# The head of a two-layer hybrid backbone: all four modulation halves on the tensor engine, strictly ordered loads, and a context projection begun with half the features

## The chip, the cores and the metric

The kernel runs on one core of a Trainium2 chip. The metric is the device time of one execution in microseconds; the median of several runs is compared. A core has a tensor engine (PE in the profile, with PEld for its weight loads), a vector engine (DVE), a scalar engine (ACT), GpSimd (POOL) and a sync engine (SP), here the issuer of nearly all transfers; 16 DMA engines carry them.

## The reference, cut to what matters

Two layers work on 1024 latent tokens with 256 context tokens in front, 1024 features each, in fp32. Layer 0 attends globally and in a window, layer 1 has a convolution and a neighbourhood attention. The change lies where layer 0 begins:

```python
m = silu(cond) @ mod_w[l] + mod_b[l]          # cond: c for latent, c_ctx for context
shift, scale, gate = split(m, 3)              # 1024 features each
h = rms_norm(x, norm_g[l]) * (1 + scale) + shift
aq, ak, av, ag, bq, bk, bv, bg = split_cols(h @ w_in, EVEN_WIDTHS)
```

`mod_w[0]` is 1024 x 3072. Before any token of layer 0 can be projected, 1024 x 2048 of it (shift and scale, 8.4 MB) are read and multiplied by two vectors.

## The kernel before, in words

Everything is kept with features on partitions: eight feature tiles of 128 (`dk` 0 to 7). Tokens come in three chunks (`CHUNKS`): chunk 0 is the context (256 tokens), 1 and 2 are 512 latent tokens each. A projection in fp32 precision is made of three matmuls (`mm3`, L319) on a high and a low part of both operands: hi x hi, hi x lo, lo x hi. The high part is a copy on ACT, the low part a subtraction on POOL or DVE (`split`, L296).

Each chunk's `h` is made in four steps. `norm_x` squares the eight tiles on ACT and adds them on DVE; `rstd_steps` (L246) sums over partitions on PE, takes the power -1/2 on POOL with a Newton step on DVE, and spreads the result over the partitions with PE (L263). `make_h` (L303) multiplies each tile by scale and norm on DVE (L308), adds the shift on ACT, and splits. `HV` says per tile whether DVE (v) or POOL (g) makes the low part.

Shift (part 0) and scale (part 1) are computed in halves of 512 features, each from four tiles of 512 KB. `mod_half` (L171) uses PE: the two condition vectors are the stationary operand, 16 instructions (L180); the row of 512 results is copied by ACT (L182), transposed by four small matmuls (L185), and DVE adds the bias (L189) and, for scale, forms `gs` (L191). `mod_half_v` (L195) multiplies and adds on DVE (L216, L221) and sums over partitions with PE (L227). The same function later makes the gate of layer 0 and the modulation of layer 1, one step per `tick` (L742) of the layer-0 projections; `solo` is true until the first QKV projection and its first gate blocks are done.

The head's order is written as a string:

```python
PLAN = 'p0mvnbwmm1h2nbhnbh'
MWR = "ABxAVx"
```

`0`, `1`, `2` load chunks, `m` and `v` are modulation halves on PE and on DVE, `n` and `b` are the norm and its spread, `w` loads the first QKV weights, `h` makes a chunk's `h`. The halves are taken in the order shift 0, shift 1, scale 0, scale 1; the second one goes to DVE. `MWR` names the buffers in which modulation weights land, in turn: A and B are the key buffers, V the value buffer of the attention that follows, x a pool of the head. `mw_tile` (L151) hands them out. `after_mod(k)` holds a transfer on its issuing queue behind the last k modulation loads. Beyond that a list scheduler with a timeline model orders each engine's instructions, with the order of the code as priority; `tc.issue_after(i)` makes what follows on i's engine stand behind i there, and makes no other engine wait.

`proj_qkv` (L792) then works through ten token blocks j of 128 (two of context, eight latent), with 24 matmuls of 384 columns each (L320 to L322), calls `tick` at `dk` 1, 4 and 7, and copies the result out on ACT; rotary steps follow on DVE (L828, L830) and POOL (L832), and `qk_tail` (L837) transposes on PE (L840).

Of the kernel before, what the change touches and what calls it, by code (L numbers as in the profile page):

```python
# [18 lines left out]
P = 128  # L19
DK = 8  # L20
# [30 lines left out]
PFB = 2  # L51
MWB, WRB = 2, 2
OHQ = 0
# [36 lines left out]
def tile_kernel(ctx: ExitStack, tc: tile.TileContext, a, out):  # L90
# [57 lines left out]

    mm0 = []

    def mw_tile():  # L151
# [19 lines left out]
    def mod_half(pool, l, part, j):  # L171

        pb = bank("pp", nm("pm"))
        c0 = part * 1024 + j * 512
        for d2 in range(4):
            w2 = mw_tile()
            mm0.append(SY.dma_start(w2, a["mod_w"][l, 2 * d2 * P : (2 * d2 + 2) * P, c0 : c0 + 512].rearrange("(d p) n -> p d n", d=2)))
            for d in range(2):
                dk = 2 * d2 + d
                PE.matmul(pb[0:2, :], csil[:, dk, :], w2[:, d, :], start=(dk == 0), stop=(dk == DK - 1))  # L180
        row = a0.tile([P, 512], F32, tag="ost", name=nm("mrow"), bufs=2)[0:2, :]
        SC.copy(row, pb[0:2, :])  # L182
        tr = bank("tr", nm("trm"))
        for i in range(4):
            PE.transpose(tr[:, 2 * i : 2 * i + 2], row[:, i * P : (i + 1) * P], ident[0:2, 0:2])  # L185
# [3 lines left out]
        VE.tensor_tensor(dst, trv, modb[:, l, o : o + 4, None].broadcast_to([P, 4, 2]), op=ALU.add)  # L189
        if part == 1:  # L190
            VE.scalar_tensor_tensor(gs[l][:, j * 4 : j * 4 + 4, :], dst, 1.0,  # L191
                                    normg[:, l, j * 4 : j * 4 + 4, None].broadcast_to([P, 4, 2]),
                                    op0=ALU.add, op1=ALU.mult)

    def mod_half_v(pool, l, part, j, conds):  # L195

        c0 = part * 1024 + j * 512
        pool, tag, bufs = (kvp, "QH", 3) if mwp[0] is not None else (pool, "macc", 2)
        accs = [pool.tile([P, 512], F32, tag=tag, name=nm("macc"), bufs=bufs) for _ in conds]
        pre = []  # L200
        for dk in range(DK):
            if solo[0] and dk % 2 == 0:
                w2 = mw_tile()
                d_ = SY.dma_start(w2, a["mod_w"][l, dk * P : (dk + 2) * P, c0 : c0 + 512].rearrange("(d p) n -> p d n", d=2))
                if mwp[0] is not None:
                    mm0.append(d_)
                pre = [w2[:, 0, :], w2[:, 1, :]]
# [28 lines left out]
    def newton_rsqrt(pool, v, n, tag):  # L236
# [7 lines left out]
        return r  # L244

    def rstd_steps(pool, accs, n, tag, inv=1.0, tr="tr"):  # L246
# [12 lines left out]
        yield  # L259
        yield  # L260
        bc = bank(tag, nm("bc"))
        for b in range(nb):
            PE.matmul(bc[:, b * P : (b + 1) * P], r[:, b : b + 1].broadcast_to([P, P]), ident, start=True, stop=True)  # L263
        return bc
# [54 lines left out]
    def mm3(o, lh, ll, rh, rl, first, last):  # L319
        PE.matmul(o, lh, rh, start=first, stop=False)  # L320
        PE.matmul(o, lh, rl, start=False, stop=False)  # L321
        done[0] = PE.matmul(o, ll, rh, start=False, stop=last)  # L322

    raws = []
# [329 lines left out]
    with ExitStack() as p0x:  # L654
        w0p = p0x.enter_context(tc.tile_pool(name="w0p", bufs=1, reuse_waits="tile"))
        W0B = 8

        def load_w0(src, u, n):
            return load_w(w0p, a[src], u * n, n, 384, W0B, rb=WRB)

        with tc.tile_pool(name="st0", bufs=1, reuse_waits="tile") as st0:
# [4 lines left out]
            def load_x(c):  # L666
# [4 lines left out]
                else:  # L671
                    t = st0.tile([P, DK, n], F32, tag=f"xr{c}", name=f"xr{c}")
                    xraw[c] = [t[:, dk, :] for dk in range(DK)]
                    for d in range(0, DK, 4):
                        SY.dma_start(t[:, d : d + 4, :],
                                     a["cT"][:, d : d + 4, :] if c == 0 else a["xT"][:, d : d + 4, 0:n])
                    return
                for dk in range(DK):
                    SY.dma_start(xraw[c][dk], a["xT"][:, dk, t0 - 256 : t0 - 256 + n])

            def norm_x(c):
                n = CHUNKS[c][1]
                acc = kvp.tile([P, 512], F32, tag="QH", name=nm("acc"), bufs=3)
                for dk in range(DK):
                    if dk == 0:
                        SC.activation(acc[:, :n], xraw[c][0], AF.Square)
                    else:
                        sq = kvp.tile([P, 512], F32, tag="QL", name=nm("sq"), bufs=3)
                        SC.activation(sq[:, :n], xraw[c][dk], AF.Square)
                        VE.tensor_tensor(acc[:, :n], acc[:, :n], sq[:, :n], op=ALU.add)  # L690
                return acc

            def norm_bc(c, acc):
                n = CHUNKS[c][1]
                return run(rstd_steps(st0, [acc], n, "st"))[:, :n]

            made = [0]
            accs, bcs, mh = [], [], [(0, 0), (0, 1), (1, 0), (1, 1)]
            mwp[0] = st0
            for ev in PLAN:  # L700
                if ev in "012":
                    with after_mod(XA):
                        load_x(int(ev))
                elif ev == "p":
                    SC.dma_start(modb, a["mod_b"])
                    SC.dma_start(normg, a["norm_g"])
                elif ev == "n":
                    accs.append(norm_x(len(accs)))
                elif ev == "w":
                    with after_mod(XA):  # L710
                        w0 = load_w0("ev_qkv", ORDER[0], 384)
                elif ev == "m":
                    mod_half(st0, 0, *mh.pop(0))
                elif ev == "v":
                    run(mod_half_v(st0, 0, *mh.pop(0), (0, 1)))
                elif ev == "b":
                    bcs.append(norm_bc(len(bcs), accs[len(bcs)]))
                elif ev == "h":
                    make_h(0, made[0], lambda dk, c=made[0]: xraw[c][dk], bcs[made[0]], h[made[0]])
                    made[0] += 1  # L720

# [921 lines left out]
```

## Time and profile before

| | |
|---|---|
| median of 3 runs | 1569.27 us (1566.07 to 1572.54) |
| profiled execution | 1571.46 us, span 1569.6 us |
| PE busy over the span | 1460.8 us (93%) |
| DVE / POOL / ACT busy | 1129.4 / 830.0 / 762.0 us |
| granted TensorE clock, mean | 0.961 |
| first QKV matmul | 47.72 us |
| first matmul of latent chunk 1 | 62.01 us |
| moved by DMA | 221.03 MB, mean 141 GB/s |

Engine names are as above; SPq and ACTq are the queues from which transfers are issued. A row of the timeline has start, duration, engine, line, operation, output and inputs, shapes and count, and in brackets how long the engine had been idle and what released it. Rows whose matmuls overlap have durations longer than the distance of their starts.

### The profile page before, as it was taken

The page shows a single profiled execution, that of the slowest core. Times are in us where ns is not written, and L with a number is a line of the kernel's source. Part 1 is how long each engine was busy: PE and PEld are TensorE (multiplying, and loading weights), DVE is VectorE, ACT ScalarE, POOL GpSimd, SP SyncE. Part 2 cuts the span into 40 slices and gives each one's busy share as a digit, 9 for nine tenths or more (in the row PEclk, how much of TensorE's full clock was granted, in tenths as well). Part 3 has the DMA queues.
Part 4 walks back from the last instruction along what each step waited for, and adds up shares of the span by engine and source line. Part 5 has one row for each costly group of instructions (what it writes and reads, how often), then busy time and mean ns, then how long its engine had stood idle before and what let it go on. Part 6 is the DMA issues. An engine that isn't in the chain of part 4 may idle for free.

```text
span 1569.6 us, 22251 instructions
## 1 busy us (share of the span) xinstructions
PE 1460.8 (93%) x6984; PEld 1178.9 (75%) x6984; DVE 1129.4 (72%) x2172; ACT 762.0 (49%) x1545; POOL 830.0 (53%) x762
## 2 busy tenths in 40 slices
PE   6989999998999999899999889999999999899995
PEld 1878877876888677588887568888887787677784
DVE  4898896797768677455488668999654466776776
ACT  2721354545454754655555746443343445545472
POOL 1561463555465675756545756665443333444575
PEclk9899999999999999999999989999999999799897
DMA  9548245424431225612112022214547888889632
GB/s 337 190 142 260 87 142 167 132 67 125 154 116 47 67 91 167 224 47 61 48 38 85 14 94 61 81 58 148 177 154 224 237 229 242 248 231 251 187 95 108
DMA packets 199438, 221.03 MB, mean 141 GB/s; under 512 B 18956, under 2 KB 155352, under 8 KB 199320
## 3 DMA queue, kind: packets, MB, share of 16 engines
q1 hardware_dynamic: 192656, 208.04, 43.5%
q10 hardware_dynamic: 6664, 11.57, 2.3%
q8 instruction: 55, 0.90, 0.2%
q14 instruction: 63, 0.52, 0.1%
HBM read 159.51 MB, written 60.03 MB: 140 GB/s over the span
## 4 chain that ended last, share of the span: by engine, by line
PE 65%; DVE 14%; DMA 11%; issue 4%; POOL 2%; SPq 2%; ACT 1%; ACTq 0%; DVEq 0%; POOLq 0%
PE p L322 6%; PE p L321 6%; PE p L320 6%; PE ov L411 4%; PE ov L413 4%; PE ov L412 4%; PE po L320 4%; PE po L321 4%; PE po L322 4%; PE st L467 4%; PE st L471 4%; DMA mw<-in_mod_w_dram 3%; DVE macc L221 2%; PE pq L322 2%; PE pq L321 2%
## 5 line engine op out<-in xcount | busy, mean ns | idle before, releaser
L301 POOL TENSOR_TENSOR pl<-pf,ph 128x512 fp32r<-128x512 f32 (+4 forms) x321 | 393.7, 1237 | 320.1 <-ACT ph L298 260.0
L301 POOL TENSOR_TENSOR wl<-wr,wh 128x256 fp32r<-128x256 f32 (+2 forms) x256 | 197.5, 788 | 203.1 <-ACT wh L298 192.4
L479 ACT ACTIVATE pf<-st 128x512 f32<-128x512 f32 x284 | 167.3, 597 | 177.4 <-PE st L471 138.3
L298 ACT CAST ph<-pf 128x512 fp32r<-128x512 f32 (+4 forms) x364 | 210.5, 588 | 28.9 <-PE ov L412 21.5
L298 ACT CAST wh<-wr 128x256 fp32r<-128x256 f32 (+2 forms) x264 | 102.8, 404 | 172.9 <-DMA wr<-in_ev_qkv_dram 40.4
L320 PE MATMUL p<-hh,wh 128*128 128x512 f32 x448 | 177.5, 398 | 2.9 <-DVE spk L301 1.5
L321 PE MATMUL p<-hl,wh 128*128 128x512 f32 x448 | 178.0, 398 | 0.2 <-POOL hl L301 0.2
L322 PE MATMUL p<-hh,wl 128*128 128x512 f32 x448 | 175.9, 400 | 0.1
L467 PE MATMUL st<-QH,KAt 128*128 128x512 f32 (+4 forms) x364 | 145.4, 401 | 11.4 <-ACT pf L479 9.7
L411 PE MATMUL ov<-ph,Vt 128*128 128x512 f32 (+4 forms) x364 | 143.5, 394 | 9.7 <-ACT ph L298 5.0
L413 PE MATMUL ov<-pl,Vt 128*128 128x512 f32 (+4 forms) x364 | 144.1, 396 | 6.8 <-POOL pl L301 3.6
L471 PE MATMUL st<-QL,KBt 68*128 68x512 f32 (+4 forms) x364 | 139.0, 391 | 5.8 <-DVE QL L390 5.7
L412 PE MATMUL ov<-ph,Vt 128*64 128x512 f32 (+4 forms) x364 | 140.5, 386 | 0.0
L1122 DVE SCALAR_TENSOR_TENSOR cps<-U,taps,cps 128x512 f32<-128x512 f32 x184 | 124.3, 748 | 0.0
L591 DVE TENSOR_REDUCE mp<-mx 128x1 f32<-128x512 f32 x128 | 85.7, 682 | 42.5 <-PE mx L590 41.8
L221 DVE SCALAR_TENSOR_TENSOR macc<-mw,csil,macc 128x512 f32<-128x512 f32 x107 | 94.5, 901 | 17.5 <-DMA mw<-in_mod_w_dram 16.7
L320 PEld LDWEIGHTS p<-hh,wh 128*128 128x128 f32 x448 | 84.6, 189 | 23.6 <-DVE spk L301 1.7
L321 PEld LDWEIGHTS p<-hl,wh 128*128 128x128 f32 x448 | 84.5, 189 | 20.4 <-POOL hl L301 0.6
L322 PEld LDWEIGHTS p<-hh,wl 128*128 128x128 f32 x448 | 84.8, 189 | 20.1 <-POOL wl L301 0.6
L467 PEld LDWEIGHTS st<-QH,KAt 128*128 128x128 f32 x364 | 71.2, 196 | 33.4 <-ACT pf L479 17.6
L413 PEld LDWEIGHTS ov<-pl,Vt 128*128 128x128 f32 x364 | 71.1, 195 | 32.5 <-POOL pl L301 7.8
L411 PEld LDWEIGHTS ov<-ph,Vt 128*128 128x128 f32 x364 | 71.3, 196 | 27.3 <-ACT ph L298 8.4
(277 smaller groups left out, 3546.2 us busy)
## 6 DMA issues: line engine op xcount, KB each, us to landing
mw<-in_mod_w_dram SPq DMA_DIRECT2D x34, 512.0 KB, 5.9
Q<-qs SPq DMA_DIRECT2D x40, 256.0 KB, 2.7
QH<-Q SPq DMA_DIRECT2D x80, 128.0 KB, 2.8
wr<-in_od_d_dram SPq DMA_DIRECT2D x64, 128.0 KB, 2.7
mw<-in_mod_w_dram SPq DMA_DIRECT2D x28, 256.0 KB, 3.3
wr<-in_ev_qkv_dram SPq DMA_DIRECT2D x32, 192.0 KB, 3.6
KAt<-KD SPq DMA_DIRECT2D x16, 384.0 KB, 6.2
wr<-in_od_wo_dram SPq DMA_DIRECT2D x48, 128.0 KB, 3.2
```

What stands on the lines that cost most here:

```text
L221: VE.scalar_tensor_tensor(t, w, csil[:, dk, q : q + 1], t, op0=ALU.mult, op1=ALU.add)
L298: SC.copy(hi, src)
L301: (GP if leng == "g" else VE).tensor_tensor(lo, src, hi.bitcast(F32), op=ALU.subtract)
L320: PE.matmul(o, lh, rh, start=first, stop=False)
L321: PE.matmul(o, lh, rl, start=False, stop=False)
L322: done[0] = PE.matmul(o, ll, rh, start=False, stop=last)
L411: PE.matmul(o, V[:, 64:192], ph[:, :n], start=(t == 0), stop=False)
L412: PE.matmul(g.ov[0:64, q0 : q0 + n], V[:, 0:64], ph[:, :n], start=False, stop=False)
L413: pvs.append(PE.matmul(o, V[:, 64:192], pl[:, :n], start=False, stop=(last and g.sink is None)))
L467: sts.append(PE.matmul(st[:, :n], KA[:, cs], g.QH[:, q0 : q0 + n], start=True, stop=False))
L471: PE.matmul(st[:, :n], KB[0:68, cs], g.QL[0:68, q0 : q0 + n], start=False, stop=True)
L479: SC.activation(pf[:, :n], st[:, :n], AF.Exp, scale=1.0 if g.bias else SCALE)
```

## The change

All four modulation halves of layer 0 now run on PE, first those of features 0 to 511 (shift, scale), later those of features 512 to 1023. Between them the context is begun: chunk 0's `h` is made for `dk` 0 to 3 (`front`), and its two token blocks run the 24 matmuls that need only those, into two PSUM banks that are kept (`begun`); `proj_qkv` goes on with `dk` 4 to 7 later, with two ticks instead of three for these blocks. Every load of the head goes through `in_turn`, which holds it behind the previous one on its queue. The QKV weights come as two groups of four, with four raw buffers instead of two. The ring of the modulation weights becomes `ABVABVxx`, eight tiles. The back features of chunks 0 and 1 are multiplied by their norm in advance (`scaled`), so that a multiply-add on DVE finishes them when scale and shift are known. `HV0` replaces `HV` in layer 0; `behind` holds PE and ACT instructions in written order around these steps. The second half's bank is "ov", a single one, instead of "pp".

```diff
-MWB, WRB = 2, 2
+MWB, WRB = 2, 4
+HV0 = ('vvvvgvgv', 'gvgvgvgv', 'gvgvgvgv')
-PLAN = 'p0mvnbwmm1h2nbhnbh'
-MWR = "ABxAVx"
-XA = 4
+MWR = "ABVABVxx"
...
+    queue = []
+
+    def in_turn(dma):
+
+        with ExitStack() as cx:
+            if queue:
+                cx.enter_context(tc.issue_after(queue[-1].ins))
+            queue.append(dma())
+        return queue[-1]
...
     def mod_half(pool, l, part, j):
 
-        pb = bank("pp", nm("pm"))
+        pb = bank("ov" if j else "pp", nm("pm"))
...
-            mm0.append(SY.dma_start(w2, a["mod_w"][l, 2 * d2 * P : (2 * d2 + 2) * P, c0 : c0 + 512].rearrange("(d p) n -> p d n", d=2)))
+            mm0.append(in_turn(lambda: SY.dma_start(w2, a["mod_w"][l, 2 * d2 * P : (2 * d2 + 2) * P, c0 : c0 + 512]
+                                                    .rearrange("(d p) n -> p d n", d=2))))
...
-            raws.append(SY.dma_start(raw[:, :nco], src[dk * P : (dk + 1) * P, c0 : c0 + nco]))
+            load = lambda: SY.dma_start(raw[:, :nco], src[dk * P : (dk + 1) * P, c0 : c0 + nco])
+            raws.append(in_turn(load) if mwp[0] is not None else load())
...
+            def scaled(c, bc, dks):
+
+                for dk in dks:
+                    last = VE.tensor_tensor(xraw[c][dk], xraw[c][dk], bc, op=ALU.mult)
+                return last
+
+            def make_h0(c, dks, bc=None):
+
+                cond = 1 if c == 0 else 0
+                for dk in dks:
+                    x = xraw[c][dk]
+                    scale, shift = gs[0][:, dk, cond : cond + 1], modT[0][:, dk, cond : cond + 1]
+                    if bc is not None:
+                        VE.scalar_tensor_tensor(x, x, scale, bc, op0=ALU.mult, op1=ALU.mult)
+                        SC.activation(x, x, AF.Identity, bias=shift)
+                    else:
+                        VE.tensor_scalar(x, x, scale, shift, op0=ALU.mult, op1=ALU.add)
+                    hi, lo = h[c][0][:, dk, :], h[c][1][:, dk, :]
+                    last = SC.copy(hi, x)
+                    (GP if HV0[c][dk] == "g" else VE).tensor_tensor(lo, x, hi.bitcast(F32), op=ALU.subtract)
+                return last
+
+            def start_qkv(w):
+
+                wh, wl = w
+                for j in range(2):
+                    begun[j] = bank("pp", nm("pq"))
+                    for dk in front:
+                        last = mm3(begun[j][:, :384], Hs(h, 0, j * P, P, dk), Hs(h, 1, j * P, P, dk), wh[dk], wl[dk],
+                                   dk == 0, False)
+                return last
...
+            front, back = range(0, 4), range(4, DK)
             mwp[0] = st0
-            for ev in PLAN:
...
+            load_x(0)
+            run(mod_half(st0, 0, 0, 0))
+            known = run(mod_half(st0, 0, 1, 0))
+            bc = norm0(0)
+            scaled(0, bc, back)
+            wf = load_w0("ev_qkv", ORDER[0], 384, front)
+            made = make_h0(0, front, bc)
+            load_x(1)
+            pq = start_qkv(wf)
+            with behind(known, made):
+                bc = norm0(1)
+            spread1 = spread[0]
+            with behind(made):
+                wb = load_w0("ev_qkv", ORDER[0], 384, back)
+            w0 = tuple({**f, **b} for f, b in zip(wf, wb))
+            made, ready = make_h0(1, front, bc), scaled(1, bc, back)
+            with behind(pq):
+                run(mod_half(st0, 0, 0, 1))
+            with behind(spread1):
+                known = run(mod_half(st0, 0, 1, 1))
+            make_h0(0, back)
+            load_x(2)
+            make_h0(1, back)
+            with behind(known, made, ready):
+                bc = norm0(2)
+            make_h0(2, range(DK), bc)
...
-                    pp = bank("pp", nm("pq"))
-                    for dk in range(DK):
+                    d0 = 4 if u == ORDER[0] and j in begun else 0
+                    pp = begun[j] if d0 else bank("pp", nm("pq"))
+                    for dk in range(d0, DK):
```

`norm0` is `norm_x` and the spread in one; `behind(...)` is `tc.issue_after` for each instruction given; `known` and `spread1` are PE instructions, `made` is one of ACT, `ready` one of DVE.

More of the change, by code (lines that the diff above doesn't have):

```diff
@@ L184, in mod_half @@
         for i in range(4):
-            PE.transpose(tr[:, 2 * i : 2 * i + 2], row[:, i * P : (i + 1) * P], ident[0:2, 0:2])
+            last = PE.transpose(tr[:, 2 * i : 2 * i + 2], row[:, i * P : (i + 1) * P], ident[0:2, 0:2])
         trv = tr[:, 0:8].rearrange("p (i c) -> p i c", c=2)
@@ L193, in mod_half @@
                                     op0=ALU.add, op1=ALU.mult)
+        return last
     def mod_half_v(pool, l, part, j, conds):
         c0 = part * 1024 + j * 512
-        pool, tag, bufs = (kvp, "QH", 3) if mwp[0] is not None else (pool, "macc", 2)
-        accs = [pool.tile([P, 512], F32, tag=tag, name=nm("macc"), bufs=bufs) for _ in conds]
+        accs = [pool.tile([P, 512], F32, tag="macc", name=nm("macc"), bufs=2) for _ in conds]
         pre = []
@@ L203, in mod_half_v @@
                 w2 = mw_tile()
[L204 to L206 removed]
+                SY.dma_start(w2, a["mod_w"][l, dk * P : (dk + 2) * P, c0 : c0 + 512].rearrange("(d p) n -> p d n", d=2))
                 pre = [w2[:, 0, :], w2[:, 1, :]]
@@ L244, in newton_rsqrt @@
         return r
+    spread = [None]
     def rstd_steps(pool, accs, n, tag, inv=1.0, tr="tr"):
@@ L262, in rstd_steps @@
         for b in range(nb):
-            PE.matmul(bc[:, b * P : (b + 1) * P], r[:, b : b + 1].broadcast_to([P, P]), ident, start=True, stop=True)
+            spread[0] = PE.matmul(bc[:, b * P : (b + 1) * P], r[:, b : b + 1].broadcast_to([P, P]), ident, start=True,
+                                  stop=True)
         return bc
@@ L322, in mm3 @@
         done[0] = PE.matmul(o, ll, rh, start=False, stop=last)
+        return done[0]
     raws = []
@@ L656, in tile_kernel, with load_w0 @@
         W0B = 8
-        def load_w0(src, u, n):
-            return load_w(w0p, a[src], u * n, n, 384, W0B, rb=WRB)
+        begun = {}
+        def load_w0(src, u, n, dks=range(DK)):
+            return load_w(w0p, a[src], u * n, n, 384, W0B, dks=dks, rb=WRB)
         with tc.tile_pool(name="st0", bufs=1, reuse_waits="tile") as st0:
@@ L690, in norm_x @@
                         VE.tensor_tensor(acc[:, :n], acc[:, :n], sq[:, :n], op=ALU.add)
[L691 to L698, printed above, removed]
-            mwp[0] = st0
-            for ev in PLAN:
[L701 to L720, printed above, removed]
@@ new lines, in norm0 @@
+                return run(rstd_steps(st0, [acc], n, "st", tr="st"))[:, :n]
+            def scaled(c, bc, dks):
[16 more added lines that the diff above has]
+                return last
@@ new lines, in start_qkv, with behind @@
+            def start_qkv(w):
[5 more added lines that the diff above has]
+                                   dk == 0, False)
+                return last
+            @contextmanager
+            def behind(*ins):
+                with ExitStack() as cx:
+                    for i in ins:
+                        cx.enter_context(tc.issue_after(i.ins))
+                    yield
@@ new lines, in tile_kernel @@
+            front, back = range(0, 4), range(4, DK)
+            mwp[0] = st0
+            SC.dma_start(modb, a["mod_b"])
+            SC.dma_start(normg, a["norm_g"])
+            load_x(0)
[9 more added lines that the diff above has]
+                bc = norm0(1)
```

9 lines of the change are left out of this document (5 added, 4 removed).

## The prediction

> **What bounds the kernel now.** I read the busy time by stage first, since the change touches only the head: the stretch up to the end of the first QKV projection. Columns after the window's length: busy us and instruction count of PE, PEld, DVE, ACT, POOL, then granted clock, DMA share and GB/s.
>
> ```profile
> core 0: us, PE busy (x) PEld busy (x) DVE busy (x) ACT busy (x) POOL busy (x), PEclk, DMA share, GB/s
> ...
> 8.90:18.80 9.90, 9.80 (x16) 1.57 (x16) 4.67 (x11) 1.47 (x6) 0.00 (x0) 1.00 1.06 375
> 18.80:23.70 4.90, 0.38 (x4) 0.32 (x4) 4.90 (x10) 2.31 (x5) 1.24 (x1) 0.76 1.05 387
> 23.70:31.20 7.50, 7.45 (x13) 1.16 (x13) 4.71 (x7) 1.01 (x2) 2.41 (x4) 0.70 0.95 325
> 31.20:41.50 10.30, 10.30 (x34) 3.03 (x33) 3.80 (x10) 4.90 (x10) 1.66 (x3) 1.00 1.04 389
> 41.50:47.70 6.20, 3.39 (x29) 3.14 (x28) 5.99 (x15) 5.92 (x14) 1.00 (x1) 0.80 1.05 383
> 47.70:55.20 7.50, 7.14 (x21) 6.31 (x22) 7.50 (x16) 4.34 (x11) 5.84 (x6) 0.50 0.98 338
> 55.20:62.00 6.80, 6.80 (x45) 6.80 (x44) 5.05 (x11) 3.88 (x7) 2.89 (x3) 0.98 0.57 173
> 62.00:78.60 16.60, 16.60 (x99) 16.08 (x99) 14.10 (x21) 12.14 (x25) 10.08 (x10) 1.00 0.08 29
> 78.60:95.30 16.70, 15.35 (x88) 14.50 (x86) 16.70 (x19) 5.15 (x12) 11.01 (x8) 1.00 0.30 90
> 95.30:110.00 14.70, 9.74 (x56) 9.22 (x56) 14.66 (x18) 4.20 (x11) 10.25 (x7) 0.89 0.60 173
> ```
>
> Until 55 us the DMA engines are full, at 325 to 389 GB/s; from 62 us on they are not, and PE and DVE share the load: DVE is busy 45.46 of the 48.0 us after 62. Then I read PE in order of time, to see what it does while the loads run.
>
> ```profile
> 8.93 9.80 PE L180 MATMUL pm<-mw,csil 128*2 128x512 f32 x16 [8.93 <-DMA mw<-in_mod_w_dram]
> 19.49 0.38 PE L185 MATMUL trm<-ident,mrow 2*128 2x2 f32 x4 [0.76 <-ACT mrow L182]
> ...
> 34.52 7.03 PE L180 MATMUL pm<-mw,csil 128*2 128x512 f32 x16
> ...
> 47.72 0.69 PE L320 MATMUL pq<-wh,hc 128*128 128x384 f32 x1 [2.01 <-ACT hc L298]
> 48.21 0.52 PE L321 MATMUL pq<-wl,hc 128*128 128x384 f32 x1
> 48.53 0.52 PE L320 MATMUL pq<-wh,hc 128*128 128x384 f32 x1
> ...
> 62.01 0.34 PE L320 MATMUL pq<-wh,hh 128*128 128x384 f32 x1
> 62.18 0.34 PE L321 MATMUL pq<-wl,hh 128*128 128x384 f32 x1
> ```
>
> One half of the modulation costs PE 9.80 us at the start and 7.03 us later (16 instructions, 0.44 us each). The first QKV matmul starts at 47.72 us. Its successors start 0.32 us apart (48.21 to 48.53), against 0.17 us at full clock (62.01 to 62.18), and the 47.70 to 55.20 window has a clock of 0.50. The context chunk ends where the first latent chunk begins, at 62.01. So the head is two things: 48 us in which PE is fed by loads, and a cold 14.3 us for the 48 context matmuls. The last view is what PE waits for from 62 to 130 us.
>
> ```profile
> PE trk L840 <- DVE qs L301: 5.2, 4, 2.8
> PE trm L227 <- DVE macc L221: 1.8, 1, 1.8
> ```
>
> Those 7.0 us are what an easier DVE could give back. Over the whole span PE has the least slack by far:
>
> ```profile
> PE 1460.8 (93%) x6984; PEld 1178.9 (75%) x6984; DVE 1129.4 (72%) x2172; ACT 762.0 (49%) x1545; POOL 830.0 (53%) x762
> ```
>
> **The change, part by part.** Durations that the steps need, as groups of the first 62 us (mean ns behind the bar):
>
> ```profile
> L690 DVE TENSOR_TENSOR acc<-acc,sq 128x512 f32<-128x512 f32 x14 | 10.8, 770 | 3.9 <-ACT sq L689 3.3
> L221 DVE SCALAR_TENSOR_TENSOR macc<-mw,csil,macc 128x512 f32<-128x512 f32 x14 | 10.6, 794 | 0.0
> L308 DVE SCALAR_TENSOR_TENSOR xr<-xr,gs,bc 128x512 f32<-128x512 f32 x6 | 4.0, 742 | 1.7 <-PE bc L263 1.7
> L690 DVE TENSOR_TENSOR acc<-acc,sq 128x256 f32<-128x256 f32 x7 | 3.7, 527 | 0.0
> L308 DVE SCALAR_TENSOR_TENSOR xr<-xr,gs,bc 128x256 f32<-128x256 f32 x8 | 3.4, 469 | 0.0
> ...
> L189 DVE TENSOR_TENSOR modT<-trm,modb 128x8 f32<-128x8 f32 x3 | 0.5, 155 | 0.0
> ```
>
> ```profile
> L689 ACT ACTIVATE sq<-xr 128x512 f32<-128x512 f32 x14 | 8.3, 620 | 0.4 <-DVE acc L690 0.2 <-DMA xr<-in_xT_dram 0.2
> L298 ACT CAST wh<-wr 128x384 fp32r<-128x384 f32 x8 | 4.0, 510 | 11.4 <-DMA wr<-in_ev_qkv_dram 11.4
> ...
> L314 ACT ACTIVATE xr<-xr,modT 128x256 f32<-128x256 f32 x4 | 1.8, 495 | 0.0
> L182 ACT COPY mrow<-pm 2x512 f32<-2x512 f32 x3 | 1.7, 569 | 6.9 <-PE pm L180 6.9
> L298 ACT CAST hc<-xr 128x256 fp32r<-128x256 f32 x4 | 1.5, 387 | 0.0
> ```
>
> *Loads.* The same bytes go out in another order: context (1.05 MB), shift and scale of features 0 to 511 (4.2 MB), four weight tiles (0.8 MB), chunk 1 (2.1 MB), four weight tiles, the other two modulation halves (4.2 MB), chunk 2 (2.1 MB). At the 375 to 389 GB/s of the full windows, 1 MB takes 2.6 us, so after the first tile at 8.93 the second modulation half is in by about 17 us, the front weights by 19, chunk 1 by 25, the fourth half by 38, chunk 2 by 43. The eight tiles of the new ring hold two halves, so the third half waits only for PE's first one, long done; the queue behind that wait is everything later, in order, and I cost it at nothing because the 4 MB already queued cover it. If that cover were gone, each missed 0.5 MB tile would be 1.4 us. Two raw weight buffers more cost nothing on an engine; they let the back weights be queued as soon as POOL has split the front ones, by about 23 us. The rotary table and the gate weights still stand behind the last four modulation tiles and are first used after 62 us.
>
> *First two halves.* PE starts at 8.93 and ends the first at 18.73 as before, then goes straight on: 7.03 gives 25.8, and two sets of small matmuls (transposes at 0.38 a set, the norm of the context) bring it to 27.0. So PE sets this, not the loads (17 us). The tail is the row copy and the transposes (18.73 to 19.87 in the rows, 1.14), and two DVE instructions of 0.155, with hand-overs 1.6 us; then the feature tile's 0.469 on DVE, 0.495 and 0.387 on ACT: first QKV matmul at about 30.0 us, 17.7 sooner than now.
>
> *Context begun.* 24 of its 48 matmuls. At full clock ACT sets the pace (0.88 per feature tile) and they end near 34; cold (0.32 each) they end at 37.7. PE has had about 3 us of little work, like the 41.50 to 47.70 window, where 3.39 us of small matmuls and a 2.01 us wait were followed by a clock of 0.50. I take 36.8. [...]
>
> *Third and fourth half.* They are put behind the begun context on PE: 36.8 + 7.0 = 43.8. The fourth stands behind the spread of chunk 1's norm as well, and needs the one "ov" bank, which ACT's 0.569 copy frees. The norm: ACT is free of the front tiles near 33, casts four weight tiles (2.0) and squares eight (5.0), to 40; with the last add (0.77), small matmuls, the power on POOL and three small DVE steps it is spread near 43 to 44. So the fourth half runs 44.6 to 51.6, transposes to 52.2, and the same tail puts the first of the remaining context matmuls at about 54.6. This is later than today's 47.72: half the work is done by then, but the one DVE-made half is now 7.0 us of PE.
>
> *Rest of the context.* 24 matmuls, 4.1 us warm, 7.7 cold; middle 5.9, done at 60.5 against 62.01. While PE waits for the second tail (2.6 us) it may take chunk 1's front features, which are ready; how far the written order allows that the trace can't show. Bounds 0 and 2.6; I take 1. So the first latent chunk is 2.5 us ahead.
>
> *DVE and chunk 2.* Gone from DVE: 16 x 0.794 = 12.7 us at most (the two multiplies that start the sums have one input less). Added: eight scaling multiplies, 4 x 0.527 + 4 x 0.770 = 5.2, since the back features are scaled by the norm before their modulation is known; and six instead of four subtractions for the context's low parts, 2 x 0.527 = 1.1. Net 6.4 less. The context's begun half also drops two of the ticks that feed later modulation, 4 x 0.794 = 3.2 us moved behind this stretch. Chunk 2's norm, whose scaling now runs in the DVE-bound stretch after 71 us, can be done by about 70, since its data lands at 43. The rows' 7.0 us of PE waits on DVE are the most this can return; its other end is nothing, as DVE is full of later modulation that moves up into any hole. I take 1.5, nearer to nothing, because that filler stays.
>
> Sum: 2.5 + 1.5 = 4.0 us. The profiled execution took 1571.46 us for a span of 1569.6; from it, 1567.5; from the median 1569.27, which I forecast, **1565**. From the head on, PE is the bound and a shift there should pass through to the end.
>
> **The rivals.** *More than that.* The clock stays up over both short gaps, PE fills the second with chunk 1, and DVE's waits go. Steps: 2.7 and 1.8 us from the two cold stretches, 1.6 more filling, 3 more of the waits: 4.0 + 9.1 = 13 at most, two thirds of it, 9, likely: 1560. For it: the clock was 1.00 from 31 to 41 us with PE busy throughout. Against: the 0.50 after a wait of 2.01. [...]
>
> *No gain, DVE ends it.* The first QKV projection ends when DVE's rope steps and filler let it, wherever the context ended: 1569. For it: 45.46 of 48.0 us busy; against: 6.4 us of DVE work are gone.
>
> *Slower: the fourth half waits for the norm of chunk 1.* Between chunk 1's first square and the spread of its norm the kernel now takes this long:
>
> ```profile
> 36.92 0.62 ACT L686 ACTIVATE acc<-xr 128x512 f32<-128x512 f32 x1
> ```
> ```profile
> 57.25 1.05 PE L263 MATMUL bc<-ident,nr 128*128 128x128 f32 x8
> ```
>
> 20.3 us, with both engines full of other work, where I count 10 to 11. From 33 that is 53.3; the fourth half then runs to 60.4, context matmuls resume at 63.4 and end at about 69.5: 7.5 us behind, 1577. With the second front (chunk 1's features and the third half's row copy on the same ACT queue) a little more. It decides from the point where the spread comes later than 46 us. Against it: ACT has nothing else but weight casts there.
>
> **How the numbers follow.** 0.5% is 7.8 us, about what a measurement of this kernel can tell from no change. Chances: the forecast 0.36; the larger gain 0.27, most of it just past the bound; no gain 0.15; slower 0.22, most of it at the bound or beyond it since the later order may shift too. That gives 0.28 faster, 0.51 within, 0.21 slower. The range takes in the larger gain with part of its excess (1556) and the slow case (1578).
>
> **What would show it.** Right: first QKV matmul near 30 us, a gap of some 3 us on PE before it, 24 context matmuls, then two unbroken halves ending near 52, and the first latent chunk at 59 to 60.5; no DVE instruction of L221's kind before 60. Wrong on the fast side: a clock of 1.00 in the stretch after 30 and latent matmuls before 57. Wrong on the slow side: a PE wait ahead of the fourth half, ended by the norm's DVE or ACT work, or holes in the DMA share before 40 us. Wrong about DVE: the context ends early, but the waits at L840 grow beyond 7 us.

## The result, and the profile after

The changed kernel took 1577.2 us (median; 1573.9 to 1580.1), the kernel before 1567.7 us beside it (1564.6 to 1572.5): a ratio of 1.0056, 95% interval 1.0032 to 1.0081. It is slower by some 9 us; the forecast was 4 us faster. Medians here and below are of each kernel's fast runs, which leaves out one run of the kernel before (2332.63 us) and two each of two kernels further down (160.42 and 161.28; 159.88 and 161.57 us).

The profiled execution after took 1573.93 us (span 1572.1), the fastest of its runs, while the one before (1571.46) was among its slower ones. So the two profiles are only 2.5 us apart, and what they show is read stage by stage, not as a sum. The busy time of PE is as before:

```profile
PE 1459.3 (93%) x6988; PEld 1178.4 (75%) x6988; DVE 1112.4 (71%) x2164; ACT 765.8 (49%) x1551; POOL 836.3 (53%) x761
```

The head by the same windows as in the prediction (busy us and count of PE, PEld, DVE, ACT, POOL, then granted clock, DMA share, GB/s):

```profile
core 0: us, PE busy (x) PEld busy (x) DVE busy (x) ACT busy (x) POOL busy (x), PEclk, DMA share, GB/s
8.90:18.80 9.90, 9.85 (x24) 2.39 (x24) 2.05 (x9) 1.10 (x4) 0.71 (x1) 1.00 1.05 385
18.80:23.70 4.90, 4.90 (x14) 0.95 (x13) 1.41 (x4) 2.10 (x5) 3.86 (x4) 1.00 1.05 386
23.70:31.20 7.50, 4.63 (x19) 2.42 (x18) 3.15 (x10) 3.36 (x9) 0.00 (x0) 0.90 0.97 305
31.20:41.50 10.30, 10.30 (x35) 5.34 (x34) 8.01 (x9) 6.07 (x13) 5.25 (x4) 0.91 1.05 388
41.50:47.70 6.20, 4.60 (x25) 2.56 (x24) 1.77 (x7) 0.75 (x2) 1.01 (x1) 0.92 1.06 380
47.70:55.20 7.50, 7.50 (x15) 1.24 (x13) 7.39 (x11) 6.60 (x12) 3.10 (x2) 0.84 0.90 328
55.20:62.00 6.80, 5.93 (x38) 5.51 (x37) 4.95 (x12) 3.21 (x7) 0.06 (x1) 1.00 0.42 134
62.00:78.60 16.60, 14.88 (x77) 14.09 (x77) 12.08 (x23) 7.96 (x18) 7.47 (x7) 0.90 0.23 72
78.60:95.30 16.70, 15.53 (x92) 15.14 (x91) 16.70 (x19) 9.33 (x19) 12.13 (x9) 1.00 0.26 73
```

PE is now busy from 9 us on but for 2.9 us between 23.7 and 31.2 and 1.6 between 41.5 and 47.7, and from 62 to 78.6 us, where it was busy without a break before, it stands still for 1.7 us. PE in order of time shows where the head lost what it won:

```profile
29.67 0.69 PE L331 MATMUL pq<-wh,hc 128*128 128x384 f32 x1 [2.21 <-ACT hc L727]
30.16 0.52 PE L332 MATMUL pq<-wl,hc 128*128 128x384 f32 x1
30.48 0.52 PE L331 MATMUL pq<-wh,hc 128*128 128x384 f32 x1
...
35.60 7.03 PE L189 MATMUL pm<-mw,csil 128*2 128x512 f32 x16
42.56 1.05 PE L263 MATMUL trs<-ones,acc 128*128 128x2 f32 x8
...
45.55 1.16 PE L273 MATMUL bc<-ident,nr 128*128 128x128 f32 x8 [1.60 <-DVE nr L251]
46.64 8.72 PE L189 MATMUL pm<-mw,csil 128*2 128x512 f32 x16
55.29 0.44 PE L331 MATMUL pq<-wh,hh 128*128 128x384 f32 x1
...
59.68 0.40 PE L195 MATMUL trm<-ident,mrow 2*128 2x2 f32 x4
60.95 1.05 PE L263 MATMUL trs<-ones,acc 128*128 128x2 f32 x8 [0.87 <-DVE acc L706]
61.91 0.44 PE L331 MATMUL pq<-wh,hc 128*128 128x384 f32 x1
...
66.72 0.45 PE L333 MATMUL pq<-wh,hc 128*128 128x384 f32 x1 [1.35 <-DVE hc L728]
```

To 42.6 us all goes as forecast or better. Then the fourth half starts at 46.64 and takes 8.72 us, its transposes stand at 59.68 behind latent matmuls (L331 with `hh`, from 55.29), and the context goes on at 61.91 instead of 54.6. PE's waits from 62 to 130 us, which an easier DVE was to give back:

```profile
PE trm L235 <- DVE macc L229: 3.0, 2, 2.6
PE pq L333 <- DVE hl L728: 1.8, 2, 1.2
PE pq L333 <- DVE hc L728: 1.4, 1, 1.4
PE pq L331 <- ACT hh L727: 0.4, 1, 0.4
PE trk L899 <- DVE modT L236: 0.3, 1, 0.3
```

That is 6.9 us. The same view of the kernel before has one row more than the two that the prediction shows, so its waits come to 7.7 us and not to 7.0:

```profile
PE pq L322 <- DVE hl L312: 0.7, 1, 0.7
```

From here on I use two marks: the first attention matmul, and the first matmul of layer 1's projection. They are the same instructions in every kernel, but the first does not stand for quite the same work: 674 matmuls are recorded ahead of it before, 651 after, 653 with two ticks alone. Before, then after:

```profile
160.06 0.70 PE L578 MATMUL mx<-KAt,QH 128*128 128x256 f32 x4 [0.42 <-DMA V<-vs]
...
929.45 0.40 PE L320 MATMUL p<-hh,wh 128*128 128x512 f32 x1
```
```profile
164.58 1.19 PE L591 MATMUL mx<-KAt,QH 128*128 128x256 f32 x4 [4.30 <-DMA KAt<-K]
...
934.99 0.48 PE L331 MATMUL p<-hh,wh 128*128 128x512 f32 x1
```

The head ends 4.5 us later than before, of which PE waits 4.3 for the first keys; layer 0 takes 770.4 us instead of 769.4; the rest of the span 637.1 instead of 640.2. At the end of the first QKV projection the distance is larger: its last matmul starts at 108.93 us, against 102.20 before.

### The profile page after: what moved, and what is told of

Read it like the earlier page. It is cut to its first block, busy times and chain, and to the rows that moved or that the text cites. A ratio compares the mean times of both kernels' runs of the same rounds, so it can differ in the third digit from the quotient of the medians.

```text
span 1572.1 us, 22248 instructions
## 1 busy us (share of the span) xinstructions
PE 1459.3 (93%) x6988; PEld 1178.4 (75%) x6988; DVE 1112.4 (71%) x2164; ACT 765.8 (49%) x1551; POOL 836.3 (53%) x761
## 4 chain that ended last, share of the span: by engine, by line
PE 71%; DVE 12%; DMA 9%; issue 3%; POOL 2%; ACT 1%; SPq 1%; DVEq 0%; ACTq 0%; POOLq 0%
PE p L331 7%; PE p L332 7%; PE p L333 7%; PE ov L424 4%; PE ov L426 4%; PE ov L425 4%; PE st L480 4%; PE st L484 4%; PE po L331 4%; PE po L332 4%; PE po L333 4%; DVE macc L229 2%; PE pq L331 2%; PE pm L189 2%; PE pq L333 2%
## 5 line engine op out<-in xcount | busy, mean ns | idle before, releaser
L492 ACT ACTIVATE pf<-st 128x512 f32<-128x512 f32 x284 | 167.5, 597 | 186.3 <-PE st L484 137.5
L331 PE MATMUL p<-hh,wh 128*128 128x512 f32 x448 | 180.5, 404 | 5.1 <-DVE spk L312 2.3
L331 PEld LDWEIGHTS p<-hh,wh 128*128 128x128 f32 x448 | 85.6, 191 | 25.5 <-issue 2.8
L229 DVE SCALAR_TENSOR_TENSOR macc<-mw,csil,macc 128x512 f32<-128x512 f32 x92 | 81.4, 901 | 27.0 <-DMA mw<-in_mod_w_dram 23.9
L426 PEld LDWEIGHTS ov<-pl,Vt 128*128 128x128 f32 x364 | 70.3, 193 | 28.1 <-POOL pl L312 9.3
L331 PE MATMUL pq<-wh,hh 128*128 128x384 f32 x256 | 88.3, 345 | 1.2 <-ACT pc L863 0.8
```

The source lines that it names most:

```text
L426: pvs.append(PE.matmul(o, V[:, 64:192], pl[:, :n], start=False, stop=(last and g.sink is None)))
L492: SC.activation(pf[:, :n], st[:, :n], AF.Exp, scale=1.0 if g.bias else SCALE)
```

## The experiments

### First: where in the change does the loss sit?

Theory H: it arises in the head. Rival D: behind the head, since the two ticks left out of the begun blocks push modulation steps into the attention. Four variants of the changed kernel, beside before at 1567.95 us.

**Latent matmuls behind the last transposes.**

```diff
+                        with ExitStack() as cx:
+                            if u == ORDER[0] and not d0:
+                                cx.enter_context(tc.issue_after(known.ins))
                             mm3(pp[:, :384], ...
```

> The changed kernel, with the QKV matmuls of the latent chunks held on PE behind the last modulation transposes, which in the changed kernel stand behind 24 of them (55.29 to 59.68 us). Theory H (the loss is made in the head: PE's written order and the fourth half bring the context's second half at 61.9 us): the context resumes at about 58, the first QKV projection ends 3 to 4 us earlier than the changed kernel's (before 106), total 3 to 5 us less, 1572 to 1574. Rival D (the head is even, the loss comes later, from modulation steps of layer 1 that moved into the attention): the head moves by these 3 us and the total stays at 1576 to 1578.

1588.9 us, 1.0131 (1.0109 to 1.0153): slower than the change itself, and than either theory had it. Attention starts at 166.8 us.

**Three ticks in the begun blocks.**

```diff
-                        if dk % 3 == 1:
+                        if dk % 3 == 1 or d0 and dk == 5:
```

> The changed kernel, with three ticks instead of two for each of the two begun context blocks, so that as many later modulation steps as before are fed into the first projection. Theory H: no change, 1575 to 1579. Rival D: the modulation of the gate and of layer 1 ends earlier again by several us, and the total falls by 4 to 6 us, to 1571 to 1573.

1582.5 us, 1.0081 (1.0055 to 1.0108), above both expectations. The third tick did not bring the time back, so D in this form falls.

**Third half on DVE again** (its loads in turn, its sums in other buffers).

```diff
-            with behind(pq):
-                run(mod_half(st0, 0, 0, 1))
+            run(mod_half_v(st0, 0, 0, 1, (0, 1)))
```

> The changed kernel, with the third half (shift, features 512 to 1023) made on DVE again, so that PE has 7.0 us less to do between the begun context and the fourth half. Theory H: the fourth half starts as soon as chunk 1's norm is spread, at about 42 instead of 46.6 us, the context resumes at about 57, total 4 to 5 us less than the changed kernel, 1571 to 1573. Rival D: 1575 to 1579, or more, since DVE gets 12 us of work back.

1581.7 us, 1.0089 (1.0065 to 1.0113). PE waits 11.1 us while DVE makes the half, and the last transposes come 11 us later than the changed kernel's 59.68 (3.4 of these stand ahead of the wait: this profile's begun context ends at 39.1 instead of 35.7). Made on DVE, the third half costs the head more than on PE:

```profile
50.17 1.87 PE L241 MATMUL trm<-one,macc 128*128 128x2 f32 x8 [11.08 <-DVE macc L235]
...
70.94 0.40 PE L195 MATMUL trm<-ident,mrow 2*128 2x2 f32 x4
```

**No context begun; the whole projection behind the last transposes.**

```diff
-            pq = start_qkv(wf)
...
+                            if u == ORDER[0]:
+                                cx.enter_context(tc.issue_after(known.ins))
```

> The changed kernel without the begun context: all QKV matmuls stand behind the last modulation transposes on PE. Theory H, in its strict form (between 29.7 and 35.6 us PE would otherwise only wait for chunk 1's norm): halves three and four end at about 49, the context runs in one go from about 52 to 61, total within 2 us of the changed kernel, 1575 to 1579. If beginning early pays at all, 4 us for the 24 matmuls and up to 4 more for a cold clock: 1581 to 1585.

1592.9 us, 1.0159 (1.0136 to 1.0182), the slowest of all and above both expectations, with a head that by the first mark is nearly as good as before's:

```profile
160.77 0.71 PE L591 MATMUL mx<-KAt,QH 128*128 128x256 f32 x4 [1.72 <-issue]
...
940.74 0.40 PE L331 MATMUL p<-hh,wh 128*128 128x512 f32 x1
```

Attention starts 0.7 us after before's, and layer 0 then takes 780.0 us instead of 769.4. So H falls too as an account of the whole: its last QKV matmul starts at 107.01 us, 4.8 later than before's, and its head timed alone (below) is 3.1 us longer, but the whole is 25 us slower. Whether the begun context costs the head anything stays open: by the mark this head is 3.8 us better than the changed kernel's (160.8 against 164.6), timed alone it is 1.8 us longer, with four modulation steps more in it.

### Second: single parts on the kernel before

Theory S: the loss behind the head comes from the order that the scheduler writes there, which any change of the head alters. Beside before at 1566.93 us.

**Two ticks for the context blocks, head untouched.**

```diff
-                        if dk % 3 == 1:
+                        if dk % 3 == 1 and (u != ORDER[0] or j > 1 or dk > 1):
```

> The kernel before with one thing altered: the context blocks of the first projection draw the next modulation step two times instead of three, as the begun blocks of the changed kernel do. All work up to 82 us (on PE up to about 130 us) stands in the same order as before, and the head costs the same. Theory S (the loss arises after the head: any change of what comes before makes the scheduler write another order for the attention of layer 0, and the sizes of its stages fit only the order of before): 1575 to 1585 us, the first QKV projection ending within 1 us of before's 102.2, and PE 8 us or more behind before's progress by 380 us. Theory H (what counts is the time of the head): 1566 to 1570, PE never more than 3 us behind.

1566.8 us, 1.0001 (0.9977 to 1.0026). No loss: not every change of the order costs.

**Strict order of the loads alone** (`in_turn` around each load of the head).

> The kernel before with the loads of the head in strict order of the text, and nothing else of the change. The loads already fill the DMA engines to 55 us, so the first QKV matmul stays within 2 us of 47.72 and the first projection ends at 101 to 104. Theory H: 1566 to 1571. Theory S: another order downstream, 1572 to 1585 with the head unchanged.

1581.9 us, 1.0082 (1.0054 to 1.0111). Both expectations had the head unchanged; it is not. With before's plan and ring, a load that waits for a buffer now holds up all behind it: over the first 62 us 280 GB/s are moved instead of 326, and attention starts 15 us late, at 175.2. Here the head's loss did come out at the end.

**All halves on PE alone.**

```diff
-PLAN = 'p0mvnbwmm1h2nbhnbh'
+PLAN = 'p0mmnbwmm1h2nbhnbh'
```

> The kernel before with the second half of the modulation on PE as well, and nothing else of the change: 7.0 us more of PE while it waits for loads, 12.7 us less of DVE. First context spread near 20 instead of 41, first QKV matmul at 44 to 49. Theory H: head 0 to 3 us earlier, 1564 to 1569. Theory S: whatever the head gives, 1572 to 1585.

1572.6 us, 1.0037 (1.0012 to 1.0061): within S's range, but with a head that lost. First QKV matmul at 43.78, attention at 164.6: 4.5 us late, and 5.6 at the end.

**The larger rings alone.**

```diff
-MWB, WRB = 2, 2
+MWB, WRB = 2, 4
-MWR = "ABxAVx"
+MWR = "ABVABVxx"
```

> The kernel before with the ring of eight modulation tiles (which takes turns with the key and value buffers) and four raw weight buffers, and nothing else of the change. Loads are queued earlier, in the same order; the first QKV matmul stays at 46 to 48 us. Theory H: 1564 to 1569. Theory S: 1572 to 1585 with the head unchanged or a little earlier.

1562.2 us, 0.9965 (0.9946 to 0.9985): the only kernel here that beats both, and below both expectations. Not by its head, though:

```profile
44.06 0.44 PE L320 MATMUL pq<-wh,hc 128*128 128x384 f32 x1 [0.70 <-ACT hc L298]
57.22 2.07 PE L263 MATMUL bc<-ident,nr 128*128 128x128 f32 x8
62.05 0.69 PE L320 MATMUL pq<-wh,hh 128*128 128x384 f32 x1 [2.76 <-ACT hh L298]
```

The context starts 3.7 us earlier, but chunk 1's norm is spread when it was before (57.22 against 57.25), PE waits 2.76 for chunk 1, and attention starts 3.3 us later, at 163.3. The time comes from behind the head: layer 0 763.2 us, the rest 634.9.

### Third: the head timed alone, and one number behind it

Theory M: the order behind the head is a matter of its own, and sets most of the loss; H stays the other.

**The cuts.** Kernels cut off behind `fill0(0, w0)`:

```diff
         for _ in fill0(0, w0):
             pass
+        SY.dma_start(out[0:P, 0:256], h[0][0][:, 0, :].bitcast(F32))
+        return
```

> The kernel before cut off behind the first projection and its first gate blocks (about 125 us of its 1570): what follows is left out, and one feature tile is written to the output. It times the head alone, without the attention behind it. Both theories: 120 to 150 us. The difference to the cut of the changed kernel tells them apart, see there.

> The changed kernel cut off at the same place, the rest left out in the same way. Theory H (the whole loss of 9.5 us arises in the head): 8 to 11 us slower than the cut of the kernel before. Theory M (the head loses what PE's progress shows at 110 us, and the rest arises behind it): 2 to 5 us slower. If the head in fact gained, as predicted: 2 us faster or better.

154.38 and 155.76 us: 1.4 us, less than the 2 to 5 that theory M expected. I take it as a lower bound, since the cut ends when DVE has done the modulation steps drawn so far, and the two cuts hold unequal numbers of them:

```profile
L221 DVE SCALAR_TENSOR_TENSOR macc<-mw,csil,macc 128x512 f32<-128x512 f32 x74 | 57.7, 815 | 0.5
```
```profile
L229 DVE SCALAR_TENSOR_TENSOR macc<-mw,csil,macc 128x512 f32<-128x512 f32 x56 | 47.5, 872 | 1.1 <-DMA mw<-in_mod_w_dram 0.6
```

Of before's 74, 14 are the DVE half; the other 60 are 4 more than after's 56, at 0.82 to 0.87 us each 3.4 us. So I estimate the cost of the changed head in these runs at 1.4 to 4.8 us, not 8 to 11.

**N0 10 instead of 9, on both kernels.**

```diff
-N0 = (9, 10, 2)
+N0 = (10, 10, 2)
```

> The changed kernel with one number of the attention of layer 0 altered: the first stretch of attention woven with gate blocks has 10 steps instead of 9 (N0). All work up to the end of the first projection stands as in the changed kernel. Theory M (the order behind the head is a matter of its own): the total moves by 3 us or more, up or down, 1566 to 1574 or 1580 to 1590. Theory H (what is lost is lost in the head): 1575 to 1579, like the changed kernel.

> The same number altered in the kernel before: 10 steps instead of 9. Head as before. Theory M: 3 to 20 us slower than before, 1570 to 1587, as its numbers stand where they served this order best. Theory H: 1566 to 1569.

On the changed kernel 1574.6 us, 1.0059 (1.0041 to 1.0077): no effect that can be told, and a time between the two ranges expected. On the kernel before 1578.4 us, 1.0063 (1.0042 to 1.0084): as large a loss as that of the whole change, with before's head.

```profile
160.97 0.64 PE L578 MATMUL mx<-KAt,QH 128*128 128x256 f32 x4
...
935.56 0.40 PE L320 MATMUL p<-hh,wh 128*128 128x512 f32 x1
```

PE's sequence in the two traces is the same to 261.8 us and parts there; layer 0 takes 774.6 us.

### Fourth: other numbers behind the changed head

> The changed kernel with one number of layer 0's attention altered (VS0, the depth from which a group's steps are shared out, 11 instead of 12); its head stands as it was. Theory M (the order behind the head sets the loss): together with the two runs r3_after_n8 and r4_after_nfill and the two known ones (1577.2 as it is, 1574.6 with N0 10) the totals spread over 8 us or more. Theory H (the head sets it): 1574 to 1580 in all of them.

> The changed kernel with N0 8 instead of 9: the first stretch of attention woven with gate blocks is one step shorter. Head as in the changed kernel. Theory M: anywhere in 1565 to 1590, see r2_after_vs. Theory H: 1574 to 1580.

> The changed kernel with 46 instead of 43 steps reckoned for the second projection when it is woven into the attention (NFILL). All up to 170 us stands as in the changed kernel. Theory M: anywhere in 1565 to 1590, see r2_after_vs. Theory H: 1574 to 1580.

VS0 is not what my expectation calls it: every VS0-th low part of the attention's exponentials is made by DVE instead of POOL, so 11 also moves a little work. Results: VS0 11 1561.9 us, 0.9981 (0.9959 to 1.0002); N0 8 1574.9, 1.0064 (1.0040 to 1.0087); NFILL 46 1576.5, 1.0063 (1.0037 to 1.0090). Two of three stayed where H wanted them. The first is some 12 us faster than the changed kernel (0.9981 against 1.0056, each beside its own runs of before), whose PE sequence it shares to 217 us, and level with before, with a head that started attention later still:

```profile
13.29 7.42 PE L189 MATMUL pm<-mw,csil 128*2 128x512 f32 x12
...
168.27 1.19 PE L591 MATMUL mx<-KAt,QH 128*128 128x256 f32 x4 [3.14 <-DMA KAt<-K]
...
928.53 0.48 PE L331 MATMUL p<-hh,wh 128*128 128x512 f32 x1
```

VS0 11 on the kernel before was not tried; it may be the better number there too.

**Three more cuts.**

> The variant with the whole context held (e4_all_held, 1592.9 us), cut off behind the first projection like c_before, the rest left out. Theory M: its head is no later than the changed kernel's, 153 to 157 against 154.4 for the kernel before, though the whole is 25 us slower. Theory H: 165 or more.

> The variant of the kernel before with the larger rings alone (b4_ring, 1562.2 us, the fastest so far), cut off behind the first projection like c_before, the rest left out. Theory M: its head is later than before's, as PE's progress shows (4 us behind at 140 us): 154 to 159 against 154.4, though the whole is 4.8 us faster. Theory H: 148 to 151.

> The changed kernel with the latent matmuls held behind the last modulation transposes (e1_tail_first, 1588.9 us), cut off at the same place, the rest left out. By PE's progress at 110 to 150 us it is 2 to 4 us behind the changed kernel. Theory M: 157 to 161 against 155.9 for the cut of the changed kernel. Theory H: 166 to 169.

157.5, 154.5 and 158.3 us. The heads of the slowest whole kernel (all held) and of the rings differ by 3.0 us, the whole kernels by some 30. H's numbers are missed by all three. Theory M's hold for the last two, though the rings' head is level with before's (154.49 against 154.38) and not later, as M had it; all held is 0.5 us above M's range, and later than the changed kernel's 155.76, where M had it no later.

### All profiles by stage

Each profiled span cut at the two marks, from the same two rows of each trace; the ratios of the totals stand beside (before's span is that of the slower execution above). Each row is a single run, and the runs of one kernel spread by 5 to 20 us.

| kernel | to attention | layer 0 | rest of span | ratio |
|---|---|---|---|---|
| before | 160.1 | 769.4 | 640.2 | 1 |
| after | 164.6 | 770.4 | 637.1 | 1.0056 |
| after, N0 10 | 167.5 | 768.4 | 636.9 | 1.0059 |
| after, VS0 11 | 168.3 | 760.3 | 630.0 | 0.9981 |
| after, N0 8 | 161.9 | 774.8 | 635.2 | 1.0064 |
| after, NFILL 46 | 162.6 | 773.6 | 632.3 | 1.0063 |
| after, tail first | 166.8 | 776.3 | 644.6 | 1.0131 |
| after, three ticks | 169.7 | 776.4 | 638.8 | 1.0081 |
| after, DVE half | 170.0 | 775.7 | 642.8 | 1.0089 |
| after, all held | 160.8 | 780.0 | 643.1 | 1.0159 |
| before, N0 10 | 161.0 | 774.6 | 640.6 | 1.0063 |
| before, two ticks | 158.7 | 765.7 | 637.0 | 1.0001 |
| before, rings | 163.3 | 763.2 | 634.9 | 0.9965 |
| before, in turn | 175.2 | 771.6 | 635.7 | 1.0082 |
| before, all on PE | 164.6 | 770.2 | 639.3 | 1.0037 |

The first column spans 16.5 us, the second 19.7, the third 14.6. Over the 15 kernels the correlation of the ratio with the start of attention is 0.22, with the start of layer 1 0.82. What is shown: the head lost instead of gaining, and another order behind an unaltered head moves the total by as much as the change did (N0 10 on the kernel before, to the slow side; VS0 11 moves the changed kernel about as far to the fast side, but moves a little work too). What stays open: how the 9 us of the changed kernel divide between the two, and which pair of instructions in layer 0 makes an order good. Its single profile, its fastest run, puts 4.5 in the head and 1.0 in layer 0, but the same head is slower in other profiles: the last QKV matmul starts at 107.9 to 108.9 us in three (after, N0 8, NFILL 46) and at 113.6 in two (N0 10, VS0 11), so in some runs the head may cost more. The last section shows where they part; the variants with three ticks, the DVE half and the tail first were profiled in the longer kind as well. The waits listed for PE in layer 0 are 40.5 us in all before, 44.1 after, 34.2 with VS0 11, 44.2 all held, each scattered over about 50 places.

## Why the prediction was wrong

**First two halves, tail:** right. First QKV matmul at 29.67, forecast 30.0.

**Loads:** right as far as PE goes. 380 to 388 GB/s in the full windows to 47.7 (305 in the one from 23.7 to 31.2), and no PE wait in the rows above is for a modulation tile. Chunk 2 was reckoned to be in by 43 us; its last tile was only issued at 41.5.

**Context begun:** right, 35.6 against 36.8. After a wait of 2.21 us the matmuls start 0.32 us apart, as taken, at a granted clock of 0.54 (29.67 to 33.40), and from 33.4 us on 0.17, at 1.00 (33.40 to 35.60). With a clock of 1.00 from the first of them, the prediction had this end near 34.

**Third and fourth half:** the first step that failed. The spread was put at 43 to 44, the fourth half at 44.6 to 51.6. Two things were missing. Chunk 1's sums over partitions (L263, 42.56) are PE's own work and stand behind the third half, so the norm's chain of POOL and DVE began only then, although DVE had its last sum ready at 40.49: spread 45.55, fourth half 46.64, 2.0 late. The prediction's own figures held this: it kept PE in the third half to 43.8, and from there the 3.0 us from sums to spread lead to 46.8, not to 43 to 44. And the fourth half was costed at 7.03, which a half took at a clock of 1.00 (34.52 to 41.50 before), though 2.5 us of small matmuls and a 1.60 us wait stand ahead of it; it took 8.72, 1.7 more, at a clock of 0.58 from 46.64 to 50.70 and 1.00 from 50.70 to 55.20: by the starts in the trace its first four gaps are 0.73 to 0.86 us, the last ten 0.43. The argument used for the begun context was not used a second time.

**The gap behind the fourth half:** wrong. I let chunk 1 fill 1 us of it. The written order puts 4.4 us of chunk 1 ahead of the four transposes (55.29 to 59.68), so scale and shift of the back features came that much later. It cost little, for those matmuls had to be done anyway: holding them back started attention at 166.8, against 167.5 for the run of the changed head with the same long first half (N0 10). In the same stretch 1.05 us of sums for chunk 2 (60.95) and waits of 0.87, 0.36 and 1.35 us stand on PE; the first was not in the working, and of waits it left 1.6.

**DVE:** 1.5 us taken, 0.8 measured (7.7 to 6.9 us of waits). The prediction's 7.0 left out one row. Of the 6.9, the 0.36 and 1.35 were already counted above; without them the waits fell by 2.5. So the size is in doubt both ways, and how much of it reached the end is not shown: from the 97th QKV matmul to the last one of the first projection the changed kernel falls back by another 3.1 us.

**Sum of the head:** 4.0 us earlier forecast. Counted by QKV matmuls, the 97th starts at 71.57 us before and at 75.20 after, 3.6 later where the forecast had 2.5 earlier. Of these 6.1 us, 2.0 and 1.7 are the fourth half's, 1.05 the sums, and 1.0 the waits above those reckoned with.

**"From the head on, PE is the bound and a shift there should pass through to the end":** the second step that failed. With N0 10 on the kernel before, a head 0.9 us late ended as a loss of 10 us (0.63%); with the rings, a head 3.3 us late ended as a gain of about 5. A shift did pass through in two others: all on PE (4.5 us late, 5.6 at the end) and in turn (15 late, 15 at the end). PE is 93% busy, but its order is written anew for every head, and the worth of that order varies more than the edit. The prediction named this only in half a sentence ("the later order may shift too"); it should have been a term of its own, with ends of some 10 us on both sides.

**The rivals:** *more than that* needed the clock to stay up over both gaps; it went down at the first (0.54 from 29.67 to 33.40), and again behind the 1.35 us wait (0.50 from 67.4 to 70.3, with starts 0.32 us apart). *Slower* had its point of decision at a spread later than 46 us, and 45.55 is short of it; the sign named for it, a PE wait ahead of the fourth half ended by the norm's DVE work, did come, with 1.60 us. Its 1577 is met, but not by its mechanism of full engines: that the range holds 1577 is luck.

## What to carry to other kernels

Where a scheduler writes the order, price an edit in two terms: the stage it touches, and the reordering of all behind it; find the size of the second by altering one number that leaves the stage alone, before reading a per cent as the edit's effect. When a moved step is costed, list every small matmul that shares its engine between it and its data, and where small matmuls and a wait stand ahead of it, use a price measured behind such work: here a half took 8.72 us behind 2.5 us of small matmuls and a 1.60 us wait, against 7.03 at a clock of 1.00. After such an edit retune the numbers behind it: one of four such settings brought the changed kernel back to the level of before.

## What the hardware showed that I had not expected

The same twelve matmuls behind the same four, in the same order and at nearly the same time, took 5.31 us in the changed kernel's profile and 7.42 in that of its VS0 variant:

```profile
8.95 3.57 PE L189 MATMUL pm<-mw,csil 128*2 128x512 f32 x4 [8.95 <-DVE acc L706]
12.46 0.67 PE L263 MATMUL trs<-ones,acc 128*128 128x2 f32 x4
13.05 5.31 PE L189 MATMUL pm<-mw,csil 128*2 128x512 f32 x12
```

The row of VS0 11 stands above (13.29, 7.42): its twelve start with five gaps of 0.81 to 0.86 us and go on with 0.43, where the changed kernel's are 0.43 apart throughout. Why the two rows differ, by 2.1 us, no run here shows: the granted clock from 8.90 to 18.80 us reads 1.00 in both profiles.

The difference then grows. In the profile of the DVE half, whose begun context starts at 31.89, the matmuls stay 0.32 us apart to 37.8, for 6 us instead of the 4 of the changed kernel. In the VS0 profile the begun context starts 2.35 us later than in the changed kernel's, and attention 3.7 us later:

```profile
32.02 0.69 PE L331 MATMUL pq<-wh,hc 128*128 128x384 f32 x1 [2.21 <-ACT hc L727]
```

Of the five profiles of that unaltered head, the three with the short first half start attention at 161.9 to 164.6 us, the two with the long one at 167.5 and 168.3. In the kernel before, PE stood idle for loads between its first two halves, 3.88 us (4.00 with N0 10); the first half took 9.80 us (9.58 with N0 10), and in the three profiles with its head attention starts within 2.3 us. Whether the idle time keeps the difference small there was not tested.
